# Two MLPs that begin with three depth blocks, first weights summed ahead, and attention copies issued in a later step

## The chip, the core and the metric

The kernel runs on one core of a Trainium2 chip. The metric is the device time of one execution, in microseconds (us). The engines have their own instruction streams and meet through semaphores: TensorE (PE) multiplies, VectorE (DVE), ScalarE (ACT) and GpSimd (POOL) work element by element, and SyncE (SP) holds the queue from which this kernel issues nearly all transfers.

## What is computed

The reference is a two-layer trunk on `x` of 1024 positions by 1024 features, in fp32:

```python
def rmsnorm(x, g):
    y = x * rsqrt(mean(x * x, axis=-1) + EPS)
    return y * g
def sqrelu_mlp(x, w_up, w_down):
    return jnp.square(jax.nn.relu(x @ w_up)) @ w_down      # w_up 1024 x 4096
# layer 0
h = h + recurrent_block(rmsnorm(h, a_norm), ...)           # gates, a scan, w_out
h = h + sqrelu_mlp(rmsnorm(h, mlp_norm[0]), w_up[0], w_down[0])
# layer 1
k, v = shared_kv(h, ...)                                   # k is normed by head
q = rmsnorm((rmsnorm(h, b_norm) @ w_q).reshape(..., 16, 64), q_norm)
h = h + chunk_band_attention(q, k, v, rel_bias) @ w_o      # 16 heads
h = h + sqrelu_mlp(rmsnorm(h, mlp_norm[1]), w_up[1], w_down[1])
```

## The kernel before

**Layout and precision.** The residual lies transposed: eight rows `j` of 128 features, each in two halves `h` of 512 positions. An fp32 product is three matmuls in a reduced format (`mm`, lines 332 to 334): each operand is first divided into a rounded part and the rest, `h` and `l` for activations (ACT rounds at L345 or, with a gain, L348; DVE subtracts at L346 or L349), `wh` and `wl` for weights (`wsplit`, L1001 and L1002). A tile of 128 x 512 is the unit everywhere.

**The MLP's products.** Up and down projections are made by a scheme with seven products in place of eight (Winograd's). For 16 quarters `q` of `w_up`, the four weight blocks A11, A12, A21, A22 (256 KB each) are loaded, POOL makes four sums of them (L1012 to L1017), and each of the seven weights is split. The seven activation operands `XT[n]` are made once (`combine`): each has four depth blocks `i`, and block `i` comes from the rows 2i and 2i+1. PE adds the products into banks of PSUM: `z` (bank `pj`) takes operand 0 and later 5, 6 and 3, `v` (bank `sc`) operand 1, `y` and `w` (bank `tp`) operands 4 and 2. A product is four depth blocks of three matmuls, 12 in all. ACT and DVE add the banks into `c11`, `c12`, `c22`. The scale of the norm, `r`, is applied to these results; it comes from a sum of squares over all rows (`Norm.add` for each row and half, `rneg`: two matmuls with ones on the parts `ah` and `al`, L357 to L364, for each half).

**The stage ahead of each MLP.** Layer 0's MLP follows the recurrent block's output projection, whose order is made by a plan with costs (`Plan`, a manual order). `FirstOut.result` adds the residual to each row (L915), squares it (L929) and adds up the squares; `combined` makes the operands of the pairs 0 to 2 in the plan's steps, and the last pair's (rows 6 and 7) come from `combine(3)`, which the tile scheduler orders together with the first products. `ahead_weights` loads and splits A11 and A12 of the first quarter in the stage before. Layer 1's MLP follows the attention's output projection (`whole`, with `first`: a load of the residual `s<-x2d` and an addition, L833, and `last`: the squares, the store `x3d<-xr`, and `combine` for a full pair). Here nothing is in a manual order: the tile scheduler places each instruction.

**The attention.** `Proj.normed` (L1262 to L1345) makes normed keys and queries for a pair of heads, split into `ev` and `lo`. The two heads lie in the two halves of the partitions, so copies by DMA move one half to the other (`od<-ev`, `od<-lo`, `ev<-lo`; for keys six of them). The third copy writes where the first one reads, and SP stands still at it until the first has landed. `made` tells the plan when the data is there (`C_DMA`, 3.8 us from the issue). The scores (L1461) of a unit are started when enough projection matmuls have been done, which the plan uses to fill PE. At the end `reload` brings heads' outputs back (`s<-od`) for the output projection.

## Time and profile before

| | |
|---|---|
| median of three runs | 2160.58 us (2159.19 to 2161.32) |
| the profiled execution | 2157.57 us, span 2155.8 us |
| granted PE clock, mean of the span | 0.989 |
| PE / DVE / ACT / POOL busy | 97% / 72% / 52% / 27% |
| PE matmuls | 9768 |
| first MLP begins, attention's first scores, second MLP begins | at about 324, 991 and 1531 us of the span |

The profile is one execution. Its views are a page of totals, a list of what each engine waited for, tables of busy time by stretch of the span, and the instructions in order of time. A name like `pj<-l,wh` gives the written and the read tiles; in brackets stands the idle time before an instruction and what ended it. The granted clock is the share of 2.4 GHz that PE had. A matmul's own length overlaps the next one's; the distance of their starts tells the rate.

### The profile page before, as it was taken

How to read it: one execution, taken by the hardware profiler on the slowest of the kernel's cores; microseconds unless marked ns; L12 is line 12 of the kernel's file. 1: busy time of each engine (PE TensorE's matmuls, PEld its weight loads, DVE VectorE, ACT ScalarE, POOL GpSimd, SP SyncE). 2: the span in 40 equal slices, each digit the busy share in tenths (PEclk: the TensorE clock that was granted, in tenths of full speed). 3: DMA queues.
4: the chain of work that ended last, by engine and by line, in shares of the span. 5: the costliest groups of instructions: out<-in, count | busy, mean ns of one | idle time of the engine just before them, and what ended most of it. 6: DMA issues, size and time to landing. Idle time of an engine off the chain costs nothing.

```text
span 2155.8 us, 29333 instructions
## 1 busy us (share of the span) xinstructions
PE 2099.2 (97%) x9768; PEld 1738.2 (81%) x9768; DVE 1543.8 (72%) x2600; ACT 1113.8 (52%) x1971; POOL 583.2 (27%) x511
## 2 busy tenths in 40 slices
PE   7999998999999999998999999989899999999999
PEld 5788786888888888887888888878788888888887
DVE  7777668777777776646777777777777777777843
ACT  5777645444334444545667667665544443444632
POOL 0122103333310000125666666650233332000000
PEclk8999999999999999999999999999999999999999
DMA  4111335444469774532333323253444444987732
GB/s 138 40 48 45 107 103 188 158 153 150 155 221 319 238 253 139 164 117 78 94 93 99 90 74 94 79 173 109 135 167 157 154 151 169 327 263 244 245 106 95
DMA packets 174584, 319.73 MB, mean 148 GB/s; under 512 B 20576, under 2 KB 22624, under 8 KB 174432
## 3 DMA queue, kind: packets, MB, share of 16 engines
q1 hardware_dynamic: 174432, 317.85, 45.3%
q8 instruction: 77, 1.26, 0.2%
q14 instruction: 75, 0.61, 0.1%
HBM read 220.26 MB, written 78.64 MB: 139 GB/s over the span
## 4 chain that ended last, share of the span: by engine, by line
PE 87%; DVE 5%; ACT 3%; issue 2%; DMA 1%; POOL 1%; SPq 0%; DVEq 0%; POOLq 0%; ACTq 0%
PE pj L332 12%; PE pj L333 12%; PE pj L334 12%; PE tp L333 6%; PE tp L332 6%; PE tp L334 6%; PE sc L334 4%; PE sc L333 4%; PE sc L332 4%; PE p L333 4%; PE p L332 3%; PE p L334 3%; PE tp L1486 2%; PE po L1514 1%; PE po L1513 1%
## 5 line engine op out<-in xcount | busy, mean ns | idle before, releaser
L332 PE MATMUL pj<-h,wh 128*128 128x512 f32 x1205 | 482.8, 401 | 2.5 <-DVE s L1064 1.0
L333 PE MATMUL pj<-l,wh 128*128 128x512 f32 x1205 | 470.7, 391 | 3.4 <-DVE l L349 3.4
L334 PE MATMUL pj<-h,wl 128*128 128x512 f32 x1205 | 470.4, 391 | 0.0
L1001 ACT ACTIVATE wh<-raw 128x512 fp32r<-128x512 f32 x350 | 219.9, 630 | 333.9 <-PE tp L333 69.4
L1002 DVE TENSOR_TENSOR wl<-raw,wh 128x512 fp32r<-128x512 f32 x350 | 277.2, 793 | 101.6 <-ACT wh L1001 98.0
L334 PEld LDWEIGHTS pj<-h,wl 128*128 128x128 f32 x1205 | 226.5, 188 | 48.5
L332 PEld LDWEIGHTS pj<-h,wh 128*128 128x128 f32 x1205 | 227.0, 188 | 45.1 <-DVE s L1064 1.8
L333 PEld LDWEIGHTS pj<-l,wh 128*128 128x128 f32 x1205 | 227.3, 189 | 42.7 <-DVE l L349 4.3
L332 PE MATMUL tp<-h,wh 128*128 128x512 f32 x569 | 223.9, 393 | 7.0 <-ACT wh L1001 4.0
L334 PE MATMUL tp<-h,wl 128*128 128x512 f32 x569 | 223.5, 393 | 1.0 <-DVE wl L1002 1.0
L333 PE MATMUL tp<-l,wh 128*128 128x512 f32 x569 | 223.8, 393 | 0.3 <-DVE l L346 0.3
L346 DVE TENSOR_TENSOR l<-raw,h 128x512 fp32r<-128x512 f32 x224 | 152.8, 689 | 31.9 <-ACT h L345 30.7
L1031 ACT ACTIVATE s<-s 128x512 f32<-128x512 f32 x128 | 80.2, 628 | 170.8 <-DVE s L1030 170.8
L345 ACT ACTIVATE h<-raw 128x512 fp32r<-128x512 f32 x224 | 137.3, 620 | 57.7 <-DMA raw<-hid 34.9
L332 PE MATMUL p<-h,wh 128*128 128x512 f32 x384 | 153.3, 399 | 10.8 <-ACT h L587 5.9
L332 PE MATMUL sc<-h,wh 128*128 128x512 f32 x418 | 162.8, 389 | 0.1
L334 PE MATMUL sc<-h,wl 128*128 128x512 f32 x418 | 162.8, 389 | 0.0
L1012 POOL TENSOR_TENSOR raw<-raw,raw 128x512 f32<-128x512 f32 x32 | 52.3, 1635 | 407.9 <-DVE wl L1002 313.8
L333 PE MATMUL sc<-l,wh 128*128 128x512 f32 x418 | 162.6, 389 | 0.0
L333 PE MATMUL p<-l,wh 128*128 128x512 f32 x384 | 153.2, 399 | 4.2 <-DVE l L683 2.4
L334 PE MATMUL p<-h,wl 128*128 128x512 f32 x384 | 151.9, 396 | 0.0
L332 PEld LDWEIGHTS tp<-h,wh 128*128 128x128 f32 x569 | 108.0, 190 | 30.4 <-ACT wh L1001 4.4
(256 smaller groups left out, 4151.0 us busy)
## 6 DMA issues: line engine op xcount, KB each, us to landing
hid<-s SPq DMA_DIRECT2D x224, 256.0 KB, 2.0
raw<-hid SPq DMA_DIRECT2D x224, 256.0 KB, 3.7
raw<-in_w_down SPq DMA_DIRECT2D x192, 256.0 KB, 3.5
raw<-in_w_up SPq DMA_DIRECT2D x130, 256.0 KB, 2.6
s<-in_w_down SPq DMA_DIRECT2D x64, 256.0 KB, 4.3
raw<-in_w_in SPq DMA_DIRECT2D x32, 256.0 KB, 2.6
raw<-in_w_kv SPq DMA_DIRECT2D x32, 256.0 KB, 3.3
od<-ev SPq DMA_DIRECT2D x48, 128.0 KB, 2.3
```

Source lines behind the costliest of these rows:

```text
L332: pe.matmul(ps, lhsT=wh, rhs=xh, start=start, stop=False, skip_group_check=more)
L333: pe.matmul(ps, lhsT=wh, rhs=xl, start=False, stop=False, skip_group_check=more)
L334: pe.matmul(ps, lhsT=wl, rhs=xh, start=False, stop=stop, skip_group_check=more)
L345: act.activation(h, src, AF.Copy)
L346: dve.tensor_tensor(l, src, h.bitcast(F32), ALU.subtract)
L1001: act.activation(wh, raw, AF.Copy)
L1002: dve.tensor_tensor(wl, raw, wh.bitcast(F32), ALU.subtract)
L1012: pool.tensor_tensor(raw[A11], raw[A11], raw[A21], ALU.add)
L1031: act.activation(out, out, AF.Square)
L1486: pe.transpose(pt[:, g * P : (g + 1) * P], sc[:, (kb - kb0) * P : (kb - kb0 + 1) * P], ident)
L1513: pe.matmul(out, lhsT=st, rhs=ph[:, off : off + wid], start=x == 0 and y == 0, stop=False)
L1514: pe.matmul(out, lhsT=st, rhs=pl[:, off : off + wid], start=False, stop=y == final)
```

## The change

The matmuls stay the same in number and kind. Four things are different.

1. **Begin of both MLPs** (`up_begin`, new, in a manual order). `z`, `v` and `y` are begun over the depth blocks 0 to 2, then the last pair's block of each follows. `combine` is now a generator that `up_begin` steps through between the products, and uses two scratch tiles and five scaled operations in place of four tiles and two copies more. The additions of the last pair's squares (four of 512 columns) stand behind the first quarter's products and the next quarter's first splits. The banks of the two sums of squares are fixed (`po`, `tp`).
2. **First weights.** In layer 0 `ahead_weights` loads all four blocks of the first quarter in the stage before, into two tiles that otherwise hold `x`, splits A11, A12 and the sum s1, and lets POOL make the four sums there; A11 and A12 are loaded once and not twice. In layer 1 `up_first` does the same ahead of the output projection's last rows (`whole`).
3. **First stage.** `combined` has one scratch tile less and a slightly other order; the squares of the last two rows leave it.
4. **Attention copies.** `move` charges each copy's issue on SP to the plan (0.55) and gives 2.4 us to its landing. The copies that overwrite what others read are issued in a later step of the plan (`yield last`), and `made` is the time of the last.

```diff
 C_DMA = 3.8
+C_ISSUE = 0.55
+C_MOVE = 2.4
...
         def rneg(self, half):
-            s = bank()
+            s = bank("tp" if half else "po")
...
     def ahead_weights():
+
         yield out_y[NF - 2,]
+        yield xs
+        yield xs
+        raw = [t[:, hs(h)] for t in (xf("raw"), xf("raw")) for h in range(2)]
+        for x in range(4):
+            dma(raw[x], w_up[0, 0, x])
+            last = plan.load(H2)
+        yield last + 2.0
+        pair = []
         for x in (A11, A12):
-            yield raws
             yield goods
             yield goods
-            raw, wh, wl = rawf(), gr("wh"), gr("wl")
-            dma(raw, w_up[0, 0, x])
-            yield plan.load(H2) + 2.0
-            act.activation(wh, raw, AF.Copy)
+            wh, wl = gr("wh"), gr("wl")
+            act.activation(wh, raw[x], AF.Copy)
             yield plan.use("act", a_(H2))
-            dve.tensor_tensor(wl, raw, wh.bitcast(F32), ALU.subtract)
-            raws.release(plan.use("dve", d_(H2)))
-            FIRST_W.append((blocks4(wh), blocks4(wl)))
+            dve.tensor_tensor(wl, raw[x], wh.bitcast(F32), ALU.subtract)
+            last = plan.use("dve", d_(H2))
+            pair.append((blocks4(wh), blocks4(wl)))
+        yield last
+        pool.tensor_tensor(raw[A11], raw[A11], raw[A21], ALU.add)
+        pool.tensor_tensor(raw[A21], raw[A21], raw[A22], ALU.add)
+        plan.use("pool", p_(H2))
+        yield plan.use("pool", p_(H2))
+        yield goods
+        yield goods
+        wh, wl = gr("wh"), gr("wl")
+        act.activation(wh, raw[A21], AF.Copy)
+        yield plan.use("act", a_(H2))
+        dve.tensor_tensor(wl, raw[A21], wh.bitcast(F32), ALU.subtract)
+        yield plan.use("dve", d_(H2))
+        pool.tensor_tensor(raw[A21], raw[A22], raw[A11], ALU.add)
+        pool.tensor_tensor(raw[A12], raw[A12], raw[A21], ALU.add)
+        plan.use("pool", 2 * p_(H2))
+        FIRST_W.extend((*pair, (blocks4(wh), blocks4(wl)), raw[A21], raw[A12], raw[A11], raw[A22]))
 
     FIRST_W = []
...
         def last(self, j, h):
             xt = self.XR[j][h]
-            self.norm.add(h, xt)
             if self.mg is None:
+                self.norm.add(h, xt)
                 self.XS[j][h] = split(xt)
                 return
             dma(self.keep[j, :, hs(h)], xt)
             self.XS[j][h] = True
+            if j >= NF - 2:
+                return
+            self.norm.add(h, xt)
             pair = j // 2
             if all(self.XS[2 * pair + b][g] for b in range(2) for g in range(2)):
-                self.combine(pair)
+                for _ in self.combine(pair):
+                    pass
 
         def combine(self, i):
 
             (x11, x12), (x21, x22) = self.XR[2 * i], self.XR[2 * i + 1]
             ga, gb = (vec[:, V_MN + self.mg, j : j + 1] for j in (2 * i, 2 * i + 1))
-            b12, b22, t1, t3 = self.scratch()
             self.XT[0][i] = split(x11, ga)
+            yield
             self.XT[1][i] = split(x21, gb)
+            yield
+            b12, t1 = self.scratch(), self.scratch()
             act.activation(b12, x12, AF.Copy, scale=ga)
-            act.activation(b22, x22, AF.Copy, scale=gb)
             dve.scalar_tensor_tensor(t1, x11, ga, b12, ALU.mult, ALU.subtract)
             self.XT[4][i] = split(t1)
-            dve.scalar_tensor_tensor(t1, t1, -1.0, b22, ALU.mult, ALU.subtract)
-            self.XT[5][i] = split(t1)
-            self.XT[2][i] = split(b22)
-            dve.tensor_tensor(t3, b22, b12, ALU.subtract)
-            self.XT[6][i] = split(t3)
-            dve.scalar_tensor_tensor(t1, x21, gb, t1, ALU.mult, ALU.add)
+            yield
+            dve.scalar_tensor_tensor(t1, x22, gb, t1, ALU.mult, ALU.add)
+            self.XT[5][i] = split(t1, -1.0)
+            yield
+            self.XT[2][i] = split(x22, gb)
+            yield
+            dve.scalar_tensor_tensor(b12, x22, gb, b12, ALU.mult, ALU.subtract)
+            self.XT[6][i] = split(b12)
+            yield
+            dve.scalar_tensor_tensor(t1, x21, gb, t1, ALU.mult, ALU.subtract)
...
+    def up_first(layer):
+
+        raw = [wload(w_up[layer, 0, x]) for x in range(4)]
+        a11, a12 = wsplit(raw[A11]), wsplit(raw[A12])
+        pool.tensor_tensor(raw[A11], raw[A11], raw[A21], ALU.add)
+        pool.tensor_tensor(raw[A21], raw[A21], raw[A22], ALU.add)
+        s1 = wsplit(raw[A21])
+        pool.tensor_tensor(raw[A21], raw[A22], raw[A11], ALU.add)
+        pool.tensor_tensor(raw[A12], raw[A12], raw[A21], ALU.add)
+        return a11, a12, s1, raw[A21], raw[A12], raw[A11], raw[A22]
+
+    def product(o, ps, n, w, start, depth=range(4)):
+        for i in depth:
+            mm(
+                ps, (w[0][:, i, :], w[1][:, i, :]), o.XT[n][i],
+                start and i == 0, i == 3, not start and len(depth) == 4,
+            )
+
+    def up_begin(o, layer, weights, get):
+
+        a11, a12, s1, r2, r4, r3, r22 = weights
+        early, late = range(3), range(3, 4)
+        z, v, y = bank("pj"), bank("sc"), bank("tp")
+        for ps, n, w in ((z, 0, a11), (v, 1, a12), (y, 4, s1)):
+            product(o, ps, n, w, True, early)
+        raw = [wload(w_up[layer, 1, x]) for x in range(4)]
+        made = o.combine(3)
+        for _ in range(3):
+            next(made)
+        s2 = wsplit(r2)
+        product(o, z, 0, a11, False, late)
+        product(o, v, 1, a12, False, late)
+        product(o, y, 4, s1, False, late)
+        next(made)
+        c11, c12, c22 = get(), get(), get()
+        act.activation(c11, z, AF.Copy)
+        product(o, z, 5, s2, False)
+        dve.tensor_tensor(c11, v, c11, ALU.add)
+        s4 = wsplit(r4)
+        act.activation(c22, y, AF.Copy)
+        next(made)
+        w = bank("tp")
+        product(o, w, 2, s4, True)
+        s3 = wsplit(r3)
+        next(made)
+        dve.tensor_tensor(c12, z, c22, ALU.add)
+        product(o, z, 6, s3, False)
+        next(made, None)
+        dve.tensor_tensor(c12, w, c12, ALU.add)
+        a22 = wsplit(r22)
+        first = wsplit(raw[A11]), wsplit(raw[A12])
+        for j in range(NF - 2, NF):
+            for h in range(2):
+                sq = gf("sq")
+                act.activation(sq, o.XR[j][h], AF.Square)
+                dve.tensor_tensor(o.norm.acc[h], o.norm.acc[h], sq, ALU.add)
+        dve.tensor_tensor(c22, z, c22, ALU.add)
+        return (z, a22, c11, c12, c22), (raw, first)
...
-    ws0 = up_weights(0, 0, FIRST_W)
-    sums0 = up_sums(ws0[0])
-    o1.combine(NF // 2 - 1)
+    with tc.manual_schedule(engines=set(ENG)):
+        begun = up_begin(o1, 0, FIRST_W, rawf)
...
     pos = Sema(plan, BANKS["po"])
     rows = Sema(plan, ROWS)
+
...
             yield plan.use("dve", c_dve(H2))
             ev, od, lo = (x.bitcast(F32) for x in (even, odd, low))
-            dma(od[OD], ev[OD])
-            dma(od[EV], ev[OD] if keys else lo[OD])
-            dma(ev[OD], ev[EV] if keys else lo[EV])
+            last = move(od[OD], ev[OD])
+            move(od[EV], ev[OD] if keys else lo[OD])
             if keys:
                 lows = gr("lo")
                 ls = lows.bitcast(F32)
-                dma(ls[EV], lo[OD])
-                dma(ls[OD], lo[OD])
-                dma(lo[OD], lo[EV])
+                move(ls[EV], lo[OD])
+                last = move(ls[OD], lo[OD])
                 self.KL[0][h], self.KL[1][h] = low, lows
+            yield last
+            last = move(ev[OD], ev[EV] if keys else lo[EV])
+            if keys:
+                last = move(lo[OD], lo[EV])
             for e, st in enumerate((even, odd)):
                 (self.K if keys else self.Q)[e][h] = st
-            self.made[kind, h].set(plan.t + C_DMA)
...
+    weights = up_first(1)
     o3.whole(OS, JP)
+    with tc.manual_schedule(engines=set(ENG)):
+        begun = up_begin(o3, 1, weights, sf)
```

In the order of the instructions this stands as follows. PE where the first MLP begins, before: `h_2485` is the last pair's part, then the third product's blocks begin, all with the first summed weight `wh_2469`.

```order
L332 MATMUL sc_2520<-h_2485,wh_2063 128x512
L333 MATMUL sc_2520<-l_2486,wh_2063 128x512
L334 MATMUL sc_2520<-h_2485,wl_2064 128x512
L332 MATMUL tp_2548<-h_2013,wh_2469 128x512
L333 MATMUL tp_2548<-l_2014,wh_2469 128x512
L334 MATMUL tp_2548<-h_2013,wl_2470 128x512
L332 MATMUL tp_2548<-h_2187,wh_2469 128x512
L333 MATMUL tp_2548<-l_2188,wh_2469 128x512
L334 MATMUL tp_2548<-h_2187,wl_2470 128x512
```

And now: the three products' early blocks end (`tp_2457<-h_2370` is the third pair's), then come the last pair's.

```order
L334 MATMUL tp_2457<-h_2190,wh_1949 128x512
L335 MATMUL tp_2457<-l_2191,wh_1949 128x512
L336 MATMUL tp_2457<-h_2190,wl_1950 128x512
L334 MATMUL tp_2457<-h_2370,wh_1949 128x512
L335 MATMUL tp_2457<-l_2371,wh_1949 128x512
L336 MATMUL tp_2457<-h_2370,wl_1950 128x512
L334 MATMUL pj_2455<-h_2493,wh_1893 128x512
L335 MATMUL pj_2455<-l_2494,wh_1893 128x512
L336 MATMUL pj_2455<-h_2493,wl_1894 128x512
L334 MATMUL sc_2456<-h_2497,wh_1904 128x512
L335 MATMUL sc_2456<-l_2498,wh_1904 128x512
L336 MATMUL sc_2456<-h_2497,wl_1905 128x512
```

The summed weight's product stands ahead of the last pair's operands, and its weight is the one split in the stage before.

SP's queue at the first queries, before: `ev_8386` and `lo_8388` are the parts of the first query (two heads, first 512 positions), `ev_8423` and `lo_8425` of the second.

```order
L241 DMA lo_8364<-lo_8341 64x512 x2
L241 DMA lo_8341<-lo_8341 64x512
L241 DMA raw_8410<-in_w_q 128x512
L241 DMA raw_8412<-in_w_q 128x512
L241 DMA od_8387<-ev_8386 64x512
L241 DMA od_8387<-lo_8388 64x512
L241 DMA ev_8386<-lo_8388 64x512
L241 DMA s_8429<-in_relb 128x640
L241 DMA od_8424<-ev_8423 64x512
L241 DMA od_8424<-lo_8425 64x512
L241 DMA ev_8423<-lo_8425 64x512
```

And now, where `ev_8378` and `lo_8380` are the first query's parts:

```order
L243 DMA raw_8406<-in_w_q 128x512
L243 DMA od_8379<-ev_8378 64x512
L243 DMA od_8379<-lo_8380 64x512
L243 DMA ev_8333<-ev_8333 64x512
L243 DMA lo_8335<-lo_8335 64x512
L243 DMA s_8424<-in_relb 128x640
L243 DMA od_8419<-ev_8418 64x512
L243 DMA od_8419<-lo_8420 64x512
L243 DMA ev_8378<-lo_8380 64x512
L243 DMA ev_8418<-lo_8420 64x512
```

The copies that wait for others (`ev<-ev`, `lo<-lo`, `ev<-lo`) moved behind the next transfers. On PE the first scores stand behind 15 more matmuls of the projections.

SP's queue at the last rows of the attention's output projection, before the second MLP: `s<-x2d` is a residual load, `x3d<-xr` the store of the sum.

```order
L241 DMA s_15269<-x2d 128x512
L241 DMA x3d<-xr_15271 128x512
L241 DMA s_15302<-x2d 128x512
L241 DMA raw_15735<-in_w_up 128x512
L241 DMA raw_15737<-in_w_up 128x512
L241 DMA x3d<-xr_15304 128x512
L241 DMA s_15335<-x2d 128x512
L241 DMA raw_15739<-in_w_up 128x512
L241 DMA x3d<-xr_15337 128x512
L241 DMA s_15368<-x2d 128x512
L241 DMA x3d<-xr_15370 128x512
```

And now:

```order
L243 DMA x3d<-xr_15206 128x512
L243 DMA s_15280<-x2d 128x512
L243 DMA s_15310<-x2d 128x512
L243 DMA s_15340<-x2d 128x512
L243 DMA s_15370<-x2d 128x512
L243 DMA x3d<-xr_15282 128x512
L243 DMA x3d<-xr_15312 128x512
L243 DMA x3d<-xr_15342 128x512
L243 DMA x3d<-xr_15372 128x512
L243 DMA raw_15720<-in_w_up 128x512
```

The last four residual loads stand ahead of the last four stores, and the next quarter's weights behind them.

## Rows read from the trace of the kernel before

**Rows 1.** The page, part 1: busy time, share of the span and instructions.

```profile
PE 2099.2 (97%) x9768; PEld 1738.2 (81%) x9768; DVE 1543.8 (72%) x2600; ACT 1113.8 (52%) x1971; POOL 583.2 (27%) x511
```

**Rows 2.** Busy time by stretch of the span; columns as its first line says.

```profile
core 0: us, PE busy (x) PEld busy (x) DVE busy (x) ACT busy (x) POOL busy (x), PEclk, DMA share, GB/s
260.00:320.00 60.00, 60.00 (x267) 49.67 (x266) 39.14 (x53) 28.11 (x43) 0.00 (x0) 1.00 0.43 144
...
320.00:360.00 40.00, 30.60 (x111) 22.46 (x110) 33.52 (x40) 21.26 (x35) 12.64 (x8) 0.87 0.49 164
360.00:980.00 620.00, 619.91 (x2734) 512.61 (x2733) 443.30 (x648) 275.43 (x475) 119.35 (x81) 1.00 0.55 186
980.00:1000.00 20.00, 12.18 (x55) 9.63 (x54) 10.76 (x21) 7.30 (x17) 6.98 (x7) 0.87 0.53 141
...
1400.00:1460.00 60.00, 54.11 (x312) 46.12 (x311) 42.64 (x117) 40.36 (x91) 30.73 (x32) 0.97 0.50 158
...
1520.00:1580.00 60.00, 53.27 (x224) 42.40 (x223) 48.19 (x70) 31.02 (x55) 11.91 (x8) 0.97 0.45 148
```

**Rows 3.** Order of time, PE, first MLP: start, length, line, [idle before, releaser].

```profile
335.83 0.72 PE L332 MATMUL tp<-h,wh 128*128 128x512 f32 x1 [4.02 <-ACT wh L1001]
...
351.86 0.50 PE L363 MATMUL tp<-ah,onesr 128*128 128x512 f32 x1 [2.94 <-ACT ah L357]
```

**Rows 4.** PE's waits: by what, us in total, times, longest.

```profile
PE sc L1461 <- DMA ev<-lo: 4.2, 1, 4.2
...
PE pj L333 <- DVE l L349: 3.4, 2, 2.9
...
PE tp L332 <- ACT s L1057: 3.0, 1, 3.0
```

**Rows 5.** Order of time at the first scores: PE, SP's queue, DVE.

```profile
990.70 0.40 PE L334 MATMUL pj<-h,wl 128*128 128x512 f32 x1
997.69 0.44 PE L1461 MATMUL sc<-ev,ev 128*128 128x128 f32 x1 [6.60 <-ACT vs L1275]
...
999.11 0.63 PE L333 MATMUL pj<-l,wh 128*128 128x512 f32 x1
999.54 0.63 PE L334 MATMUL pj<-h,wl 128*128 128x512 f32 x1
...
987.54 3.44 SPq L241 DMA_DIRECT2D lo<-lo  x3
...
992.13 0.47 SPq L241 DMA_DIRECT2D od<-ev  x1
...
995.43 0.46 SPq L241 DMA_DIRECT2D ev<-lo  x1
...
986.04 0.68 DVE L1323 TENSOR_TENSOR lo<-q,ev 128x512 fp32r<-128x512 f32 x1
```

**Rows 6.** Order of time, first MLP: DVE, then ACT, then POOL.

```profile
324.85 1.22 DVE L915 TENSOR_TENSOR xr<-p,xr 128x1024 f32<-128x1024 f32 x1
...
336.19 1.76 DVE L1002 TENSOR_TENSOR wl<-raw,wh 128x512 fp32r<-128x512 f32 x1
...
339.55 0.68 DVE L1002 TENSOR_TENSOR wl<-raw,wh 128x512 fp32r<-128x512 f32 x1
...
328.91 0.62 ACT L345 ACTIVATE h<-sc 128x512 fp32r<-128x512 f32 x1
...
335.84 1.56 POOL L1015 TENSOR_TENSOR raw<-raw,raw 128x512 f32<-128x512 f32 x1 [0.72 <-DVE wl L1002]
```

**Rows 7.** Order of time, before the second MLP: SP's queue, then DVE.

```profile
1534.81 0.43 SPq L241 DMA_DIRECT2D s<-x2d  x1
...
1538.30 0.69 DVE L833 TENSOR_TENSOR xr<-tp,s 128x512 f32<-128x512 f32 x1 [1.35 <-DMA s<-x2d]
```

**Rows 8.** Order of time near the attention's end: SP's queue, then PE.

```profile
1402.37 10.29 SPq L241 DMA_DIRECT2D s<-od  x5
...
1418.03 0.80 PE L1461 MATMUL sc<-ev,ev 128*128 128x512 f32 x1 [4.15 <-DMA ev<-lo]
```

More of the change, by code (lines that the diff above doesn't have):

```diff
@@ L896, in scratch @@
         def scratch(self):
-            return [t[:, hs(h)] for t in (xf("sc"), xf("sc")) for h in range(2)]
+            return gf("sc")
         def loads(self):
@@ L990, in combined @@
             self.first[i,].set(plan.t)
-            for _ in range(4):
+            for _ in range(3):
                 bs.release(plan.busy["dve"] + LAT)
@@ L1003, in wsplit, with up_weights @@
         return blocks4(wh), blocks4(wl)
-    def up_weights(layer, q, first=None):
+    def up_weights(layer, q):
         raw = [wload(w_up[layer, q, x]) for x in range(4)]
-        if first is None:
-            first = wsplit(raw[A11]), wsplit(raw[A12])
-        return raw, first, wsplit(raw[A22])
+        return raw, (wsplit(raw[A11]), wsplit(raw[A12])), wsplit(raw[A22])
     def up_sums(raw):
@@ new lines, in product @@
+    def product(o, ps, n, w, start, depth=range(4)):
[12 more added lines that the diff above has]
+        made = o.combine(3)
+        for _ in range(3):
+            next(made)
[28 more added lines that the diff above has]
+        return (z, a22, c11, c12, c22), (raw, first)
@@ L1023, in mlp_up @@
+    def mlp_up(o, layer, begun):
         R = []
-        def product(ps, n, w, start):
-            for i in range(4):
-                mm(ps, (w[0][:, i, :], w[1][:, i, :]), XT[n][i], start and i == 0, i == 3, not start)
         def relu(out, src, h, op):
@@ L1031, in relu @@
             act.activation(out, out, AF.Square)
+        (z, a22, c11, c12, c22), ahead = begun
         tail = None
         for q in range(NQ + 1):
-            if q < NQ:
-                raw, (a11, a12), a22 = up_weights(layer, q) if ws is None else ws
-                ws = None
+            if 0 < q < NQ:
+                if q == 1:
+                    raw, (a11, a12) = ahead
+                    a22 = wsplit(raw[A22])
+                else:
+                    raw, (a11, a12), a22 = up_weights(layer, q)
                 z, v = bank("pj"), bank("sc")
-                product(z, 0, a11, True)
-                product(v, 1, a12, True)
+                product(o, z, 0, a11, True)
+                product(o, v, 1, a12, True)
                 c11 = sf()
@@ L1048, in mlp_up @@
                 break
-            s1, s2 = up_sums(raw) if sums is None else sums
-            sums = None
-            y = bank("tp")
-            product(y, 4, s1, True)
-            product(z, 5, s2, False)
-            if not R:
-                R.extend((o.r(0), o.r(1)))
-            c12, c22 = sf(), sf()
-            act.activation(c22, y, AF.Copy)
-            dve.tensor_tensor(c12, z, c22, ALU.add)
-            s4, s3 = wsplit(raw[A12]), wsplit(raw[A11])
-            w = bank("tp")
-            product(w, 2, s4, True)
-            dve.tensor_tensor(c12, w, c12, ALU.add)
-            product(z, 6, s3, False)
-            dve.tensor_tensor(c22, z, c22, ALU.add)
+            if q:
+                s1, s2 = up_sums(raw)
+                y = bank("tp")
+                product(o, y, 4, s1, True)
+                product(o, z, 5, s2, False)
+                c12, c22 = sf(), sf()
+                act.activation(c22, y, AF.Copy)
+                dve.tensor_tensor(c12, z, c22, ALU.add)
+                s4, s3 = wsplit(raw[A12]), wsplit(raw[A11])
+                w = bank("tp")
+                product(o, w, 2, s4, True)
+                dve.tensor_tensor(c12, w, c12, ALU.add)
+                product(o, z, 6, s3, False)
+                dve.tensor_tensor(c22, z, c22, ALU.add)
+            else:
+                R.extend((o.r(0), o.r(1)))
             relu(c11, c11, 0, ALU.max)
@@ L1069, in tail @@
             def tail(q=q, z=z, a22=a22, c11=c11, c12=c12, c22=c22):
-                product(z, 3, a22, False)
+                product(o, z, 3, a22, False)
                 dma(hid[0, q], c11)
@@ L1246, in tile_yoco_rglru_chunk_attention, with move @@
     rows = Sema(plan, ROWS)
+    def move(dst, src):
+        dma(dst, src)
+        return plan.use("sp", C_ISSUE) + C_MOVE
     class Proj:
```

34 lines of the change are left out of this document (17 added, 17 removed).

## Prediction

> **What bounds the kernel now.** I read the engine shares first. TensorE (PE) is busy 97% of the span [rows 1], and the change leaves its 9768 matmuls as they are, so only what PE loses between them can be won. Where it loses shows in the table of stretches [rows 2]. Between 360 and 980 us it is busy 619.91 of 620 us with 2734 matmuls, 0.2268 us each: this is the full rate, at a granted clock of 1.00 (2.4 GHz). Four short stretches fall behind it. Counting their matmuls at 0.2268 us, 320 to 360 loses 40 - 111 x 0.2268 = 14.8 us and 1520 to 1580 loses 60 - 224 x 0.2268 = 9.2 us: these are the starts of the two MLPs. In 980 to 1000 and in 1400 to 1460, where small products are mixed in, PE is idle 7.8 and 5.9 us: the first scores of the attention, and a place near its end.
>
> Then the list of PE's waits and the order of time tell what ended last there. At 335.83 the third product of the first MLP had waited 4.02 us for its weight, the first sum of weight blocks, and at 351.86 the sum of squares had waited 2.94 us for `ah` [rows 3]. At the second MLP `pj` waited 2.9 us, the longer of two such waits, for the last pair's `l`, and a `tp` product 3.0 us for a buffer that ScalarE reads late (`s` of L1057) [rows 4]. The first scores waited 6.60 us. The list names ACT `vs`, but PE goes on only after SP's copy `ev<-lo`, issued at 995.43 for 0.46 us, has landed [rows 5]. Near the end it was a copy `ev<-lo` too, 4.2 us [rows 4].
>
> After a long wait PE is slow as well: behind the 6.60 us, matmuls start 0.43 us apart (999.11 to 999.54) [rows 5], the clock's lower level (1.2 GHz), and the stretches with waits have clocks of 0.87 to 0.97 [rows 2]. A wait costs more than its length, and one removed gives that back.
>
> **The change part by part.**
>
> *First MLP.* Before, PE does `z` and `v` whole and then needs the first summed weight, which POOL makes only now (335.83). After, that sum and its split are made in the stage ahead, and PE begins with three depth blocks of `z`, `v` and `y`: 27 matmuls x 0.2268 = 6.1 us that need nothing of the last pair. In that time DVE and ACT must make the last pair's first three operands. In the trace the pair's last addition starts at 324.85 and takes 1.22 us, to 326.1 [rows 6]; PE has finished the stage's products by then, so its 27 end at 330.4 to 331. The steps behind the addition are: two DVE subtractions (0.6 apart), one scaled subtraction (0.68), an ACT rounding (0.62) and a DVE subtraction (0.68) [rows 6]: 1.2 + 0.68 + 0.62 + 0.68 = 3.2, and some 0.3 for four hand-overs, to 329.6. So there is no wait, with 0.8 to 1.4 us to spare. The 9 late matmuls and three products of 12 (2.7 us each) follow. I went on so, row by row in the changed order: a second operand and a second weight split for each 2.7 us of PE, some 2.6 us of DVE. That is tight, and I count 0.1 + 0.1 + 0.6 us of small waits there.
>
> Then comes what is not removed: the four additions of the last pair's squares now stand behind all this, in the time of the next weights' sums on POOL. A DVE subtraction in SBUF that meets a POOL addition (335.84, 1.56 us) takes 1.76 us, the same one alone 0.68 [rows 6]. With the additions slowed in that way, `ah` for the first sum of squares comes some 2.2 us after PE asks, the second some 1.5 us. That leaves 0.8 + 2.2 + 1.5 = 4.5 us, and 0.5 for a slower clock behind it: 5.0 instead of 14.8, **9.8 us won**. Bounds: 11.5 if the sums of squares are not waited for more than before at a full clock, 6 if both are followed by half-rate stretches of 3.4 us or the tight steps slip by one DVE step each.
>
> *Weights ahead.* Two more 256 KB loads, one split and four POOL additions move into the stage at 260 to 320. PE is busy 60.00 of 60 us there, DVE 39.14 [rows 2]. The cover is this DVE slack of 21 us. Four POOL additions could each lengthen one DVE operation by 1.76 - 0.68 = 1.1 us [rows 6], 4.3 us in all: nothing on the path while the cover lasts, 4.3 us if it doesn't. I take 0.5, bounds 0 and 4.3. The loads pass the output weights on SP.
>
> The Trainium skill speaks against this part (SBUF — State Buffer, the rule on the shared port pair): a GpSimd operation and a DVE operation with two SBUF inputs exclude one another for the whole instruction. The 1.76 us agree with it. By that rule alone the summing moved ahead would only move the blocking; the sum above differs because DVE has slack where it is moved to.
>
> *Second MLP.* The same begin, with 9.2 us to win. Here the pair's additions came late for another reason: each residual load `s<-x2d` stood behind a store that waits for the addition before it. The last was issued at 1534.81, and the addition ran at 1538.30 [rows 7]. In the changed order the four loads stand together ahead of the four stores, so the additions follow PE's column by one DVE step. The weight sums are made during the products before. I count no wait up to the next quarter's weights, and 3.5 us (3 to 4, as in the first MLP less its 0.8) at the sums of squares: **5.7 us won**, bounds 3 and 8. What is taken for this is buffers: four raw and six split tiles are held through the last output weights, whose loads must then be on time; that is the lower bound.
>
> *Attention, first scores.* Before, SP does the key's dependent copies in place and stands still for each: three `lo<-lo` from 987.54 take 3.44 us, and the first query's `od<-ev` is issued only at 992.13, its `ev<-lo` at 995.43 after another wait [rows 5]. After, dependent copies stand later in the queue. The first query's parts are there at 986.7 [rows 5]; its last copy then stands behind the second query's two, so it is issued at about 990. With the 2.3 us that the copy of 995.43 took to be used, it lands at 992.5. The planner also puts 15 more matmuls ahead of the scores: 990.70 + 16 x 0.2268 = 994.3. So nothing is waited for: 6.8 us of wait (990.9 to 997.69) and the slow matmuls behind it, 6 x (0.43 - 0.23) = 1.2 and some 0.6 for the scores, 8.6 in all. I take **7.5**, as planned scores elsewhere get less fill; bounds 3 (another copy or its split comes last) and 8.6.
>
> *Attention, the rest.* All heads' copies and fill are re-planned, with SP's issue time in the plan. The one large wait left, 4.2 us with 10.29 us of SP held by five reloads `s<-od` ahead of the copies [rows 8], has its copies behind those reloads in the new order as well. I take **1.5 us won** there. Bounds: 5.9 (wait and half-rate stretch gone) and a loss of 5 (one more such wait).
>
> **The sum.** 9.8 + 5.7 + 7.5 + 1.5 - 0.5 = 24.0, and I take off 1 for the first stage's changed order: 23. The profiled execution took 2157.57 us (span 2155.8), 3 us under the median 2160.58, so this is 2134.6 in its terms and 2137.6 in those of the median. I forecast **2137 us**. Its own range, the bounds added in quadrature (3.8, 2.7, 4.5, 6.5 and 3.8), is plus or minus 10: 2127 to 2147.
>
> **The rivals.**
>
> *Blocked additions (chance 0.18).* The shared DVE and POOL time decides at both MLPs. For: the splits at 336.19 took 1.76 us, PE waited 2.94 us for `ah` at 351.86 [rows 3, 6], and the moved additions of squares now stand exactly there. Against: the chain ahead is shorter by the first sums. Each MLP would then keep two waits of about 3 us, each with a slow stretch of about 1.5: 9 us instead of 5.0 and 3.5. The gain falls by 4 + 5.5 = 9.5, to 13.5: 2147. The skill's rule on the shared pair, named above, points this way.
>
> *The copies do not bring it (0.12).* The first scores wait for something else than SP: the split or the query's norm, as the list's `vs` would have it. Then only the MLPs win, 15.5 - 1.5 = 14: 2146.5. For: the list names ACT. Against: PE starts when the copy lands.
>
> *Slower: copies come late (0.06).* A query's last copy now waits for a later step of the plan and stands behind whatever SP has got in between, above all the reloads `s<-od` that held SP for 10.29 us. Where PE comes first, it costs what it cost at 1418: 4.2 us and, as an estimate from the 1.8 at the first scores, 1.6 for a slow stretch, 5.8 us [rows 4, 8]. There are eight steps of two heads. The other parts win 15.5 + 7.5 - 1.5 = 21.5, so it decides from four such waits; with five (29 us) it is 2160.6 + 7.5 = 2168. Against: the plan now has the copy's time and sets the scores behind it, and the first place shows the distance made longer.
>
> *It does nothing or nearly so (0.04).* The hand-written begin makes PE wait in its small steps for as much as it did before, and the scores only move their wait: 2158.
>
> **How the numbers follow.** My forecast has 0.60; the rivals 0.18, 0.12, 0.06 and 0.04. The range is to reach both middle rivals, with a bound of a few us: 2126 to 2152. About 0.2% (4.3 us) is what a measurement of this kernel can tell from no change. Faster by more: nearly all of the first three cases, 0.88. Within: 0.06. Slower: 0.06.
>
> **What would show it.** In the changed profile: no wait before the first `tp` product of either MLP, and 320 to 360 with about 150 matmuls where it had 111; a wait of 1 to 3 us at each L365 product; the last four `s<-x2d` issued one behind the other; no wait at the first L1556 score, and clock 1.00 in that stretch; between 1380 and 1440 at most one wait over 3 us. I would be wrong if the waits at L365 grow to more than 3 us each, if waits of DMA `ev<-lo` appear at several heads, or if PE is idle between 200 and 320.

## The result

The changed kernel takes 2140.26 us (median, 2139.84 to 2141.76) against 2160.37 us of the kernel before: a ratio of 0.9908 (95% interval 0.9891 to 0.9926), 20.1 us less. I had forecast 2137, with a range of 2126 to 2152. The two profiled executions, 2157.57 and 2141.76 us, are 15.8 us apart; one lies 3 us under its median, the other 1.5 us above, so what is counted in the profiles has to come to 15.8 and not to 20.1.

The page of the changed kernel, part 1, and its table of stretches (the changed kernel is earlier by what it has won, so the last stretches are moved by 10 to 15 us against [rows 2]):

```profile
PE 2092.7 (98%) x9768; PEld 1732.8 (81%) x9768; DVE 1544.4 (72%) x2602; ACT 1106.4 (52%) x1965; POOL 577.2 (27%) x511
```

```profile
core 0: us, PE busy (x) PEld busy (x) DVE busy (x) ACT busy (x) POOL busy (x), PEclk, DMA share, GB/s
260.00:320.00 60.00, 60.00 (x267) 49.67 (x266) 42.11 (x54) 26.40 (x39) 3.89 (x2) 1.00 0.41 136
320.00:360.00 40.00, 37.91 (x158) 30.19 (x157) 30.02 (x42) 21.39 (x38) 8.27 (x6) 0.96 0.32 105
320.00:375.00 55.00, 51.16 (x215) 40.72 (x214) 44.88 (x62) 28.44 (x51) 13.14 (x9) 0.97 0.45 152
970.00:990.00 20.00, 18.23 (x86) 14.62 (x85) 15.79 (x25) 10.79 (x22) 12.12 (x12) 1.00 0.63 163
1390.00:1450.00 60.00, 53.04 (x288) 43.09 (x287) 42.63 (x115) 37.57 (x86) 32.68 (x32) 0.97 0.44 140
1505.00:1565.00 60.00, 54.77 (x237) 43.73 (x236) 49.06 (x70) 30.84 (x54) 12.30 (x8) 1.00 0.43 140
```

Counted as in the prediction, at 0.2268 us for each matmul, 320 to 375 loses 55 - 215 x 0.2268 = 6.2 us; the kernel before had 177 matmuls in the same 55 us and lost 14.9. At the second MLP 60 - 237 x 0.2268 = 6.2 us are lost, where [rows 2] gave 9.2. At the first scores PE is idle 1.8 of 20 us, at a clock of 1.00, where it was 7.8 at 0.87. Near the attention's end it is idle 7.0 of 60 us, where it was 5.9. So: 8.7 us won at the first MLP, 3.0 at the second, some 7 to 8 at the first scores with their clock, and a loss of about 1 near the end, with a clock of 0.97 both times. That is some 18 us, over 2 more than 15.8. The rest was lost elsewhere: at 320 us the changed kernel has begun four matmuls fewer than the kernel before (1254 and 1258, 0.9 us), and between 375 and 970 us it begins 2618 where the kernel before began 2624 (1.4 us).

What PE waits for now (by what, us in total, times, longest):

```profile
PE po L365 <- ACT ah L359: 4.0, 2, 2.0
PE pj L334 <- DVE s L1116: 3.6, 2, 1.8
...
PE po L1609 <- DVE pl L1591: 2.8, 3, 1.9
...
PE sc L1556 <- DVE t L1560: 1.9, 2, 1.7
...
PE tp L365 <- ACT ah L359: 1.3, 1, 1.3
...
PE sc L1556 <- DMA ev<-lo: 0.5, 1, 0.5
```

The wait for the first weight sum, the waits for the last pair's `l` and the 6.60 us at the first scores [rows 3 to 5] are gone; the copy `ev<-lo` costs 0.5 us. In their place stand the sums of squares (2.0 us at each MLP, 1.3 at one second half), and a new one: 1.8 us at each MLP for a bank `pj` that DVE has not yet read (L1116).

The begin of the first MLP in the changed kernel's timeline (start, busy time, operation; in brackets the idle time before it and what ended that). DVE, with the last pair's additions and the four additions of squares:

```profile
324.00 2.58 DVE L948 TENSOR_TENSOR xr<-p,xr 128x1024 f32<-128x1024 f32 x2 [4.97 <-PE p L336]
...
343.14 4.68 DVE L1107 TENSOR_TENSOR acc<-acc,sq 128x512 f32<-128x512 f32 x4
```

POOL, with its first two weight sums for the next quarter:

```profile
342.70 1.68 POOL L1044 TENSOR_TENSOR raw<-raw,raw 128x512 f32<-128x512 f32 x1 [75.18 <-DVE wl L1036]
344.45 1.62 POOL L1045 TENSOR_TENSOR raw<-raw,raw 128x512 f32<-128x512 f32 x1
```

ACT, which makes `ah` from the sums of squares, and PE, which waits for it:

```profile
347.25 0.63 ACT L359 ACTIVATE ah<-acc 128x512 fp32r<-128x512 f32 x1 [2.99 <-DVE acc L1107]
```

```profile
347.94 0.50 PE L365 MATMUL po<-ah,onesr 128*128 128x512 f32 x1 [2.01 <-ACT ah L359]
```

And the stretches of five microseconds from there on:

```profile
343.00:348.00 5.00, 2.99 (x14) 2.13 (x12) 5.00 (x6) 2.01 (x5) 2.99 (x2) 1.00 0.00 0
348.00:353.00 5.00, 5.00 (x15) 3.97 (x16) 3.16 (x5) 2.48 (x5) 2.87 (x2) 0.66 0.21 56
353.00:358.00 5.00, 5.00 (x23) 4.08 (x23) 4.85 (x9) 4.23 (x9) 0.19 (x1) 1.00 0.55 172
```

The last pair's additions end at 326.6 and PE goes through the next 88 matmuls, seven products and more, without a wait. The four additions of squares (L1107) start at 343.14, half a microsecond after POOL's first sum. They take 4.68 us (2.49 in a run without POOL's work, below); `ah` follows, and PE has stood for 2.01 us. In the next stretch the granted clock is 0.66, a mean between 1.2 and 2.4 GHz; in the one after it is back at 1.00.

That fall of the clock is no fixed part of the picture. The run e1 (below) leaves this MLP as it is. There PE stood for 2.02 us at the same place, the clock stayed at 1.00, and PE then stood at the second sum too. The stretches of e1, then its second wait:

```profile
320.00:375.00 55.00, 49.79 (x215) 39.47 (x214) 44.80 (x62) 28.35 (x50) 12.81 (x9) 1.00 0.45 152
348.00:353.00 5.00, 4.92 (x22) 4.05 (x22) 3.15 (x5) 2.47 (x6) 2.88 (x2) 1.00 0.18 56
```

```profile
354.65 0.50 PE L365 MATMUL tp<-ah,onesr 128*128 128x512 f32 x1 [1.29 <-ACT ah L359]
```

Both kernels do 215 matmuls from 320 to 375 us: the slow clock took the place of the second wait and cost nothing on top of it.

### The profile page after: what moved, and what is told of

It is laid out like the page before. It is cut to its first block, busy times and chain, and to the rows that moved or that the text cites. A ratio compares the mean times of both kernels' runs of the same rounds, so it can differ in the third digit from the quotient of the medians.

```text
span 2140.0 us, 29346 instructions
## 1 busy us (share of the span) xinstructions
PE 2092.7 (98%) x9768; PEld 1732.8 (81%) x9768; DVE 1544.4 (72%) x2602; ACT 1106.4 (52%) x1965; POOL 577.2 (27%) x511
## 3 DMA queue, kind: packets, MB, share of 16 engines
q8 instruction: 77, 1.26, 0.2%
## 4 chain that ended last, share of the span: by engine, by line
PE 86%; DVE 6%; ACT 3%; DMA 2%; issue 2%; SPq 1%; POOL 0%; DVEq 0%; POOLq 0%; ACTq 0%
PE pj L334 11%; PE pj L335 11%; PE pj L336 11%; PE tp L334 6%; PE tp L336 6%; PE tp L335 6%; PE sc L336 4%; PE sc L335 4%; PE sc L334 4%; PE p L335 4%; PE p L334 3%; PE p L336 3%; PE tp L1581 2%; PE po L1609 2%; PE po L1608 1%
## 5 line engine op out<-in xcount | busy, mean ns | idle before, releaser
L1036 DVE TENSOR_TENSOR wl<-raw,wh 128x512 fp32r<-128x512 f32 x349 | 269.8, 775 | 100.3 <-ACT wh L1035 96.5
```

The costliest lines, as they stand in the source:

```text
L1036: dve.tensor_tensor(wl, raw, wh.bitcast(F32), ALU.subtract)
```

## Experiments

Ratios are to the kernel before on the same chip; the kernel before had medians of 2160.40, 2160.33 and 2158.30 us in the three groups of runs.

### The copies: taken out, and alone

`e1_old_copies` puts the copies back in one step, `e2_only_copies` gives the kernel before these copies and nothing else.

```diff
-            last = move(od[OD], ev[OD])
...
-            yield last
-            last = move(ev[OD], ev[EV] if keys else lo[EV])
+            dma(od[OD], ev[OD])
+            dma(od[EV], ev[OD] if keys else lo[OD])
+            dma(ev[OD], ev[EV] if keys else lo[EV])
...
-            self.made[kind, h].set(last)
+            self.made[kind, h].set(plan.t + C_DMA)
```

> The changed kernel with the attention's copies as before: all issued in one step, SP's time not in the plan. Theory (the copies bring the 7.9 us that the stretch of the first scores lost less, and cost 2.5 us near the attention's end): PE waits about 6.6 us at the first scores again, and the time is 2144 to 2148 us. Rival (the MLPs and the first stage bring all of it, and the first scores would have been reached without a wait anyway): 2139 to 2142 us.

> The kernel before with the copies of the change alone. Theory: the first scores' wait of 6.6 us is gone or under 1 us, the end of the attention loses 2 to 3 us more than before, both MLP beginnings lose 15 and 9.6 us as before; 2153 to 2157 us. Rival (the wait only moves, the new order of the whole attention gives it back): 2159 to 2162 us.

Measured: 2149.64 us (0.9954, interval 0.9941 to 0.9966) and 2151.92 us (0.9964, 0.9950 to 0.9977). The copies bring 9.4 us where they are taken out and 8.5 us alone, more than the theory's 5.4; both times lie just outside its ranges (2144 to 2148 and 2153 to 2157), on the side of a larger effect. PE's waits in e1, with the one at the first scores back:

```profile
PE sc L1554 <- ACT vs L1368: 6.8, 1, 6.8
...
PE sc L1554 <- DMA ev<-lo: 4.1, 1, 4.1
```

The rivals (other parts bring all of it, or the wait only moves) are out. The 4.1 us near the attention's end are back too, so the change had removed that wait as well.

### First weights: summed in the MLP again

`e6_sums_not_ahead` keeps the three-block begin of the first MLP, but loads and sums its first weights there (its `c` tiles come from another pool).

```diff
+            raw = [wload(w_up[layer, 0, x]) for x in range(4)]
+            pool.tensor_tensor(raw[A11], raw[A11], raw[A21], ALU.add)
+            pool.tensor_tensor(raw[A21], raw[A21], raw[A22], ALU.add)
...
+            s1 = wsplit(r1)
+            product(o, y, 4, s1, True, early)
```

> The changed kernel with the first MLP's first weights as before: A11 and A12 are split in the stage ahead, the four blocks are loaded (A11 and A12 a second time) and summed by POOL when the MLP begins. The three depth blocks of `y` stand at their place behind those of `z` and `v`. Theory (without the sums ahead the three-block begin has only 18 products to do, 4.1 us, and then waits for the first sum, as the kernel before did): PE waits 6 to 8 us at the first `y` product, a half-rate stretch follows, 2147 to 2151 us. Rival (the blocks begun early are what counts, the sums come in time): 2140 to 2143 us.

Measured: 2149.61 us (0.9958, 0.9945 to 0.9972). The time and the wait are those of the theory. The wait before the first `y` product (PE, in order of time):

```profile
338.21 0.79 PE L334 MATMUL tp<-h,wh 128*128 128x512 f32 x1 [6.72 <-ACT wh L1013]
```

Everything in e6 comes later, its wait for the bank `pj` at 379.93 (1.81 us), so the stretch has to be longer than the one above. From 320 to 400 us, the kernel before, the changed kernel and e6:

```profile
320.00:400.00 80.00, 70.60 (x287) 55.58 (x286) 66.21 (x84) 37.95 (x64) 26.29 (x17) 0.94 0.52 174
```
```profile
320.00:400.00 80.00, 75.91 (x322) 60.77 (x321) 67.45 (x91) 39.87 (x70) 23.25 (x15) 0.98 0.51 175
```
```profile
320.00:400.00 80.00, 68.10 (x285) 53.59 (x284) 59.61 (x81) 35.45 (x62) 23.91 (x16) 0.96 0.49 165
```

The changed kernel does 35 matmuls more than the kernel before (7.9 us), e6 two fewer. Beginning with three blocks brings nothing here without the sum made ahead; all that was won at the first MLP needs the summing ahead. The other way round, the sums ahead with the old begin, was not tried.

### The second MLP: its begin undone

`e5_layer1_old` and `e12_layer1_old_banks` give the second MLP the scheduler's begin; in e12 the sums of squares also have their banks from the ring, as before.

```diff
-            if j >= NF - 2:
+            if j >= NF - 2 and self.mg == 0:
                 return
...
-    weights = up_first(1)
     o3.whole(OS, JP)
-    with tc.manual_schedule(engines=set(ENG)):
-        begun = up_begin(o3, 1, weights, sf)
+    mlp_up(o3, 1, None)
```

> The changed kernel with the second MLP's begin as before (scheduler's order, squares and operands of the last pair where the pair is complete, first weights not ahead). Theory (the begin of the second MLP brings its part by itself, 2.7 us by the two profiles): 2142 to 2144.5 us, PE waits 2.9 us for the last pair's `l` and 3 us for a `tp` bank again. Rival (my forecast's 5.7 us were right and the profile hides it): 2145 to 2147 us.

> As e5_layer1_old, with the banks of the second MLP's sums of squares from the ring as before; e5 had them fixed and waited 6.7 us at the second sum, which the kernel before did not. Theory (the profiles' count, 9.6 us lost there before and 7.0 after, so 2.7 us of gain): 2142 to 2144 us. Rival (my forecast's 5.7 us): 2145 to 2147 us.

Measured: 2146.71 us (0.9934, 0.9921 to 0.9948) and 2146.84 us (0.9942, 0.9930 to 0.9955): 6.5 us and about 7 us more than the changed kernel, as the rival had it. But neither is the kernel before at that place. The waits of e12 there:

```profile
1526.32 0.59 PE L335 MATMUL pj<-l,wh 128*128 128x512 f32 x1 [3.22 <-DVE l L351]
...
1540.77 0.79 PE L365 MATMUL tp<-ah,onesr 128*128 128x512 f32 x1 [4.70 <-ACT ah L359]
```
```profile
1500.00:1560.00 60.00, 50.65 (x206) 39.74 (x205) 46.34 (x66) 29.73 (x51) 10.89 (x7) 0.94 0.41 140
```

It loses 60 - 206 x 0.2268 = 13.3 us, where the kernel before lost 9.2: the 3.22 us are like its 2.87, the 4.70 for `ah` it did not have. So 6.5 us is what the begin is worth to the changed kernel, 3.0 us what the two profiles show against the kernel before. Why the old begin costs 4 us more beside the other changes was not tried.

### The sums of squares: POOL taken away, then another place

`e3_no_sums_q1` leaves out POOL's sums for the second quarter; `e4_squares_between` puts each addition of squares into a gap of DVE in `combine`; `e7_squares_and_parts` also makes `ah` and `al` right there; `e11_parts_earlier` has both `al` ahead of the next quarter's first split, which releases POOL. First e3's edit:

```diff
-                s1, s2 = up_sums(raw)
+                s1, s2 = (wsplit(raw[A21]), wsplit(raw[A22])) if q == 1 else up_sums(raw)
```

Then one of e4's places in `combine` (`sq()` makes a square on ACT, `add()` adds the one before on DVE), and e11's two:

```diff
             act.activation(b12, x12, AF.Copy, scale=ga)
+            sq()
             dve.scalar_tensor_tensor(t1, x11, ga, b12, ALU.mult, ALU.subtract)
+            add()
             self.XT[4][i] = split(t1)
...
         s3 = wsplit(r3)
+        o.norm.ready[0] = parts(o.norm.acc[0], True)
...
-        a22 = wsplit(r22)
+        o.norm.ready[1] = parts(o.norm.acc[1], True)
         first = wsplit(raw[A11]), wsplit(raw[A12])
+        a22 = wsplit(r22)
```

> The changed kernel without the POOL sums of the second quarter (q = 1) in both MLPs: four additions of weights are left out, so the products of that quarter use unsummed weights. Theory (the four additions of squares take 4.68 us instead of 2.4 because POOL's sums meet them): they take 2.4 us, the waits of 2.0 us before both first sums of squares shrink to under 0.5 us and the half-rate stretch behind them goes; 3 to 5 us less at each MLP at most, 2131 to 2136 us. Rival (their place in DVE's order decides, POOL costs nothing there): the waits stay over 1.5 us, 2138 to 2141 us.

> The changed kernel with each of the four additions of squares put into a gap of DVE between a scaled subtraction and the split that waits for ACT's rounding (four gaps of 0.70 to 0.76 us in the changed profile), at both MLPs. Theory (the gaps hold them, an addition alone takes 0.6 us): `ah` is there before PE asks, the waits of 2.0 us before the first sums go and so do the half-rate stretch behind them and the waits of 1.3 to 1.8 us later; 2131 to 2135 us. Rival (each addition delays the operand behind it, and PE waits at the four products instead): 2138 to 2144 us.

> As e4_squares_between, and the parts `ah` and `al` of both sums of squares are made right behind the next quarter's first two weight splits, the split of the first quarter's last weight behind them. In e4 the first sum of squares waited 0.2 us, but the second 1.7 us in each MLP, for an `ah` that stood behind POOL's sums on ACT's queue. Theory (only the place of `ah` and `al` in the two queues is left): waits at both sums under 0.5 us, 2 to 3 us less than e4 at each MLP, 2131 to 2134 us. Rival (DVE is full there and the 0.6 us of each `al` come out again at the products of the next quarter): 2136 to 2139 us.

> As e7_squares_and_parts, but both `al` stand ahead of the next quarter's first weight split, so that POOL's sums, which that split releases, cannot meet them. In e7 the second sum of squares still waited 1.9 us for `al` in each MLP. Theory: both waits go, 1.5 to 2 us less than e7 at each MLP, 2131 to 2134 us. Rival (the 0.6 us come out again at that split, for which PE then waits): 2135 to 2137 us.

Measured: e3 2134.13 us (0.9881, 0.9867 to 0.9894), e4 2137.73 (0.9896, 0.9883 to 0.9910), e7 2135.69 (0.9885, 0.9872 to 0.9899), e11 2132.06 (0.9875, 0.9862 to 0.9889). In e3, where POOL is still, the four additions (DVE):

```profile
344.81 2.49 DVE L1107 TENSOR_TENSOR acc<-acc,sq 128x512 f32<-128x512 f32 x4
```

2.49 us and not 4.68, and no wait before the sums of squares is left among PE's longer ones: POOL's work is the cause of the long additions and of that wait. The whole is 6.1 us shorter than the changed kernel, some 3 us for each MLP; a little of that may come from the splits, which in e3 wait for no sum. The rule of the Trainium skill that the prediction named (SBUF — State Buffer, "Who interferes with whom") says that a DVE operation with two SBUF inputs and a GpSimd operation that reads SBUF take turns for whole instructions. These runs agree: 4.68 against 2.49 us. By that rule alone, moving sums ahead would only move the blocking. For the first sums it did not, since 260 to 320 stayed full (60.00 of 60); for the additions that came to stand beside the next sums it did. e4 moved the additions out of POOL's way without leaving work out, but came between theory and rival: the first sum waited 0.2 us, the second still 1.7 at the first MLP, for an `ah` behind POOL's sums on ACT's queue, and 1.6 at the second, for `al`. e7 makes both early and came between theory and rival too: now the second `al` meets POOL. DVE's two `al` at the first MLP in e7's timeline, and PE's wait behind them:

```profile
341.33 0.69 DVE L361 TENSOR_TENSOR al<-acc,ah 128x512 fp32r<-128x512 f32 x1
...
343.64 1.75 DVE L361 TENSOR_TENSOR al<-acc,ah 128x512 fp32r<-128x512 f32 x1
```

```profile
345.45 0.50 PE L366 MATMUL tp<-al,onesr 128*128 128x512 f32 x1 [1.85 <-DVE al L361]
```

The same two on DVE in e11:

```profile
336.65 0.68 DVE L361 TENSOR_TENSOR al<-acc,ah 128x512 fp32r<-128x512 f32 x1
...
342.61 0.68 DVE L361 TENSOR_TENSOR al<-acc,ah 128x512 fp32r<-128x512 f32 x1
```

In e11 both are 0.68 us long and PE waits at neither sum. The stretch of the second MLP, in e11 first and then in the changed kernel:

```profile
1500.00:1580.00 80.00, 77.60 (x337) 62.51 (x336) 69.56 (x98) 40.27 (x71) 22.75 (x14) 1.00 0.52 169
```
```profile
1500.00:1580.00 80.00, 74.77 (x324) 59.83 (x323) 66.19 (x93) 39.96 (x69) 18.83 (x12) 1.00 0.47 154
```

e11 loses 80 - 337 x 0.2268 = 3.6 us, the changed kernel 6.5; two waits for a bank are left in e11 (0.65 us at 1556.79, 1.35 at 1569.31). At the first MLP a wait of 2.45 us for a weight split appeared at 354.65, as e11's rival had it: from 320 to 400 e11 does 334 matmuls and e7 335, where the changed kernel did 322. So e11 has won 2.7 to 2.9 us at each MLP, at the first no more than e7, and as times the two can't be told apart (0.9875 and 0.9885, intervals of 0.0014 to either side). e11 beats both kernels: its ratio of 0.9875 is 0.0033 under that of the changed one, about 7 us.

### The residual load near the attention's end

In the changed kernel SP stands at five reloads, and the load of a residual for the output projection comes behind them; DVE waits for it, and behind DVE PE. The changed kernel's timeline, SP's queue first:

```profile
1410.03 8.91 SPq L243 DMA_DIRECT2D s<-od  x5
1419.90 0.32 SPq L243 DMA_DIRECT2D s<-x2d  x1
```

Then DVE, whose addition takes the residual, and PE, which waits for what DVE makes after it:

```profile
1422.88 0.69 DVE L857 TENSOR_TENSOR xr<-pj,s 128x512 f32<-128x512 f32 x1 [3.58 <-DMA s<-x2d]
```

```profile
1424.28 0.58 PE L1609 MATMUL po<-pl,vs 128*128 128x256 f32 x1 [1.87 <-DVE pl L1591]
```

`e8_early_residual` issues that load at the begin of the column's products, `e10_residual_other_pool` does so with a tile of the large pool (`g`, not `s`), `e9_both` is e7 with e8.

```diff
+                        if k == 0:
+                            xo = o3.resid_load(j, h)
                         yield split_o[k, h]
...
-                            o3.first(ps, j, h)
+                            o3.first(ps, j, h, xo)
```

> The changed kernel with the residual loads of the attention's first output columns issued at the begin of their products and not at the end. In the changed profile DVE stands 3.58 us before such an addition for its load, which SP issued only after five reloads (8.91 us), and the weights of the products of values behind it on DVE make PE wait 1.87 us and run slowly after. Theory (that load is the cause of the loss near the attention's end): DVE's wait of 3.58 us goes, PE loses 2 to 5 us less between 1380 and 1440, 2135 to 2138 us. Rival (DVE or POOL are late there anyway, or the reload of a head is): 2139.5 to 2142 us.

> As e8_early_residual, but the residual's tile comes from the large pool of 66 tiles and not from the ten `s` tiles. In e8 DVE's wait of 3.58 us for the load was gone, but ACT then stood 5.50 us before writing an `s` tile. Theory (the early load took a tile that the attention needed): without that PE loses 2 to 4 us less near the attention's end than the changed kernel, 2136 to 2138.5 us. Rival (the late heads are late for another reason): 2139.5 to 2143 us.

> e7 and e8 together. Theory (two separate places, so the gains add): the sum of both, 2126 to 2132 us. Rival (one of them is nothing): the time of the other.

Measured: e8 2142.95 us (0.9912, 0.9899 to 0.9926), e10 2138.23 (0.9905, 0.9890 to 0.9920), e9 2135.31 (0.9884, 0.9870 to 0.9897), the time of e7 alone, as its rival had it. e8 missed its theory, and its rival by a little; e10 lies in its theory's range. In e8 ACT stood instead, before it wrote one of the ten `s` tiles, of which the early load held one; in e10 DVE's addition waits for PE, no longer for a load. ACT in e8:

```profile
1420.07 0.59 ACT L1623 ACTIVATE s<-po 64x512 f32<-64x512 f32 x1 [5.50 <-PE tp L1586]
```

DVE in e10:

```profile
1418.78 0.69 DVE L862 TENSOR_TENSOR xr<-pj,g 128x512 f32<-128x512 f32 x1 [1.43 <-PE pj L336]
```

The stretch near the end, in e10 first and then in the changed kernel:

```profile
1385.00:1445.00 60.00, 55.92 (x316) 45.80 (x314) 46.25 (x120) 40.09 (x91) 33.50 (x32) 1.00 0.43 141
```
```profile
1385.00:1445.00 60.00, 53.31 (x287) 43.43 (x286) 42.26 (x113) 36.98 (x85) 30.94 (x31) 0.97 0.44 140
```

PE is busy 2.6 us longer in e10's stretch, with 29 matmuls more. As times the two can't be told apart: 0.9905 and 0.9908, with intervals of 0.0015 to either side. In the changed kernel PE's two longest waits there were the 1.87 us above and 1.72 us at 1411.81, behind another such addition that stood for its load (0.42 us, at 1410.79); in e10 no wait of PE in this stretch is over 0.8 us. So these loads are the cause of those waits, of the second in part; what removing it brings to the whole was not settled, and that a held tile caused e8's wait rests on e10 alone.

## Why the prediction held, point by point

**The number.** 2137 was forecast and 2140.26 measured, 23 us less and 20.1. In the two profiles, where parts can be counted, it is 23 and 15.8: 1.1 us less than forecast at the first MLP, 2.7 at the second, 2.6 at the attention's end, and 1.4 lost from 375 to 970, for which the sum had no term. So the mechanism was right at the three large places and most sizes were too hopeful; that the medians are only 3 us apart is in part luck, since the profiled executions lie 3 us under and 1.5 us above theirs, and nothing shows which part those 4 us belong to.

**What bounds it** held: PE is busy 98%, and what was won is PE's waiting, with the slow clock behind it.

**First MLP** (9.8 us forecast, 8.7 counted). The begin is as worked out: additions at 326.6, no wait through seven products. The wait for the first `ah` was put at 2.2 us and is 2.01, for the reason given; e3 shows POOL, e11 the cure. The small waits (0.8 forecast) are none. The second sum (1.5) and the slow clock (0.5) stood in the sum as two terms; the runs show one or the other, a slow clock of 5 x 0.34 = 1.7 us here and a wait of 1.29 in e1. One term was not seen: 1.8 us for a bank, where DVE's next operations meet POOL again, two of 1.78 us (364.34 and 366.04), ahead of the reading of `pj` (L1116). In e3, which leaves POOL's sums at that place as they are, this wait stays (1.80 us); that POOL causes it is read from the overlap and was not tried by itself. My walk ended at the sums of squares, 15 us too early.

**Weights ahead** were costed at 0.5 us: 260 to 320 is as full as before, 60.00 of 60, and with the 1 us for the first stage it is 0.9 measured for 1.5. What the step brings, I had not separated from the begin; e6 did.

**Second MLP** (5.7 forecast, 3.0 by the profiles, 6.5 by undoing). The additions do follow PE's column, as the four loads issued together show, with DVE's first addition behind PE. The changed kernel's timeline, SP's queue and DVE:

```profile
1505.19 1.87 SPq L243 DMA_DIRECT2D s<-x2d  x4
```

```profile
1518.69 0.69 DVE L857 TENSOR_TENSOR xr<-sc,s 128x512 f32<-128x512 f32 x1 [3.18 <-PE sc L336]
```

But 3.5 us of leftover were 6.2: 2.02 and 1.26 at the sums and 1.82 for the bank, 5.1 in all. The clock was 1.00 there, so the rest is no slow clock; it goes at the edges of the waits, where a matmul ends 0.39 us after its start and the next one would have started after 0.23. The sums were sized rightly; the term at fault is the bank, which the sum did not have.

**First scores** (7.5 forecast). The stretch lost some 7.5 us less and the copies as a whole bring 8.5 to 9.4. The step that was wrong is the slack: I had the copy land 1.8 us ahead of PE, and it landed 0.5 us behind.

**The attention's end** (1.5 won forecast, about 1 lost). The direction was wrong, within the bound of 5. The wait of 4.15 us at `ev<-lo` went, as hoped, but six waits of 0.44 to 1.87 us, 6.3 in all, stand between 1390 and 1450 in its place. I had looked for the copies behind the reloads; what came late behind them is the residual load, and I had not gone through the queue for it.

**Rivals.** Blocked additions stood in the forecast and, larger, in the rival. With 6.2 us left at each MLP the runs lie between the two: nearer the forecast at the first (5.0 against 9), halfway at the second (3.5 against 9). The copies did bring their part; no late copy shows at the heads (one wait of 0.5 us).

## What to carry to other kernels

When the wait that ended last is taken away, walk the new order on past the place where it was, up to the next one or two stages: here what was left at both MLPs came from work that the change had pushed behind, into the time of another engine's work. A step that no product needs soon still wants a gap of its own: the same four additions cost some 3 us at each MLP in POOL's time (e3), and with them in DVE's gaps no product ahead of the sums waited over 0.3 us (e4). Stretches that are compared must be long enough for the late waits of the slower kernel: up to 375 us e6 is eight matmuls ahead of the kernel before (185 and 177), up to 400 us two behind. And a transfer moved ahead holds its tile for longer: out of a ring of ten tiles it moved the wait to ACT, which wanted the next one (e8), out of the large pool it did not (e10).

## What the runs showed of the hardware

A DVE operation with two operands in SBUF that meets POOL's additions took 1.75 to 1.79 us in place of 0.68, four of them 4.68 in place of 2.49 when POOL did not run; the prediction had the single one from the row, and the four together agree. A PE wait of 2.01 us was followed by five microseconds at a granted clock of 0.66 at the first MLP, one of 2.02 us by a clock of 1.00 at the second; in e1, with 2.02 and 2.00 us, it was the other way round. So a wait of this length did not settle the clock, and at the first MLP 215 matmuls were done in the same 55 us either way.
